# Identity matmuls behind the first 24 TensorE steps of the attention, and two blocks prepared ahead of its cycles in place of four

## The chip, the cores and the metric

The kernel runs on one core of a Trainium2 chip. A core has a matrix engine (TensorE, PE in the profile, with its weight loads listed apart as PEld), a vector engine (VectorE, DVE), a scalar engine (ScalarE, ACT), a general engine (GpSimd, POOL), and a queue that issues most of the DMAs (SyncE, SP). Each works through a list of instructions in order; semaphores make one wait for another. TensorE's clock is throttled and released again by the chip while a program runs; the profile has the granted share in a column PEclk, where 1.00 is the full clock. The metric is device time in microseconds, the median of several executions; lower is better.

## The reference, cut to what matters

The program is one layer of an encoder over 4096 tokens of 1024 features: an RMSNorm, one wide projection, a sparse attention, a pooling branch, gates, and an output projection. The change lies in the attention, which follows an indexer that picks 256 keys for every query:

```python
def block(i):                       # 32 blocks of 128 queries
    iscore = sum_h(relu(qi_h @ ki.T) * wi_h)          # indexer
    iscore = where(key_chunk <= q_chunk, iscore, -inf)
    idx = top_k(iscore, 256)
    s = (q @ k[idx].T) * HEAD_DIM ** -0.5             # 8 heads of 64, 2 key/value heads
    s = where(valid, s, -inf)
    o = softmax(s) @ v[idx]
```

The kernel computes the attention over all keys up to the block's own, with a bias of -1e30 where a key was not picked, which gives the same sums.

## The kernel before, in words

The program has phases: the projection to queries, keys and indexer terms, the indexer with the rest of the projections beside it (until about 2104 us), the attention (2107 us on) and the output phase. In the attention a *unit* is one block of 128 queries and one of the two key/value heads, 64 units in all, and block b has (b + 2) // 2 pairs of key tiles. Scores are formed with a high and a low part of queries and keys, in three products.

What has to be ready before a unit's first softmax tile:

- `keys(b, ...)` loads the rows of two key blocks (`k`). For the first ten blocks TensorE transposes them in one step of eight transposes (`turn_both`, through the helper `turn`, L345), and ScalarE and then VectorE copy them out of PSUM to `kh` and `kl` (`share`, L1273).
- `queries(b, ...)` loads the rows of the queries (`q`) and a copy of the bias (`bis`). In `turn_part` TensorE transposes eight heads in one step; blocks 0 to 3 have two such steps, and each is copied out by ScalarE and then VectorE to `qh` and `ql` (L1273). Block 4 and the later ones have one, and two DMAs move the rest.
- `maxima(u, t, ...)` multiplies queries and keys once (L1441, `ps` or `st`), VectorE takes the maximum of each row (L1450) into `mf`, copies it to `mz` (L1465), and `turn_maxima` has TensorE transpose it (four transposes into `pt`, L345); ScalarE puts it into `qm` (L1488). The softmax subtracts it.

Then come, for each pair of tiles, `softmax` (the logits in four products, L1509, into `st`), `weigh` (VectorE adds the transposed bias, L1522, into `tt`; ScalarE takes the exponential, L1521), `values` (L1561, into `pv`), and GpSimd's running sum of the weights.

The transposes, the first maxima and the logits share one PSUM ring, `st`, of two buffers; a step of TensorE that writes a buffer waits until the other engines have read what was in it. `ps` has one buffer. `pv` has two halves of one bank.

The order of the work is not the scheduler's of the framework. The code declares steps (`Plan.add`) with an engine, an estimated cost, a key and what they follow; `Plan.run` plays a clock with these costs, and each time an engine is free it takes the ready step with the smallest key whose buffers have room. The instructions are written out in the order in which this picks them. All steps of TensorE in the attention go through `chain`, which ties each to the one declared before it (`last_pe`), so that TensorE's order is the order of the declarations. Before the main loop, a short loop declares keys, queries and maxima of the first four blocks (`for b in range(min(WB, QB))`, QB = 4), with keys from -100 on; the main loop then declares whatever comes due, cycle by cycle.

Of the kernel before, what the change touches and what calls it, by code (L numbers as in the profile page):

```python
# [43 lines left out]
WB = 10  # L44
# [7 lines left out]
CHF = 0.16  # L52
TB = 8
MX = 8
FD = 4
FE = 2
AL = 10
# [3 lines left out]
QB = 4  # L61
# [71 lines left out]
class Plan:  # L133
# [11 lines left out]
    def new(self, name, role=None):  # L145
        return Tile_(name, role)
# [104 lines left out]
class K:  # L251
# [898 lines left out]
    def phase_attention(self):  # L1150
# [17 lines left out]
        v, act, pe, gp = nc.vector, nc.scalar, nc.tensor, nc.gpsimd  # L1168
# [27 lines left out]
        pl = Plan()  # L1196
        new = pl.new
# [15 lines left out]

        def chain(cost, key, fn, after=(), new=(), use=(), form=0):

            last_pe[0] = pl.add("pe", cost, key, fn, [*after, last_pe[0]], new, use, form)
            return last_pe[0]

        def wide(b):

# [6 lines left out]
        def landed(key, after, use):  # L1227

            s = pl.add("dma", 0.01, key, lambda: None, [after])
            return pl.add("nil", 0.0, key - 500, lambda: None, [s], use=use)  # L1230

        def keys(b, base):

            k4 = new("k4")

            def load():
                two = slice(b * P, (b + 2) * P)
                sp_dma(k4.t.rearrange("p t g c -> p t (g c)").bitcast(F32),
                       self.hlD[two, H_K:H_QI].rearrange("(t p) c -> p t c", p=P))

            def load_values():
                sp_dma(vv[:, b:b + 2], self.rowD[slice(b * P, (b + 2) * P), R_V - R_QI:].rearrange("(t p) c -> p t c", p=P))
            ld = pl.add("dma", 0.8, base - 8, load, use=[k4])
            VV[b // 2] = pl.add("dma", 0.5, base + 9, load_values, [ld])
            if b < WB:
                turn_both(b, k4, ld, base + 1)
                return
            k4.users += 2
            for n in range(2):
                turns.append((base + 1 + n, lambda n=n: turn_keys(b, n, k4, ld, base + 1 + n)))  # L1250

        def turn_both(b, k4, ld, key):

            s = wide(b)
            cols = slice(b // 2 * P, b // 2 * P + P)
            half = [slice(0, 64), slice(64, P)]

            def turn():
                for n in range(2):
                    for i in range(2):  # L1260
                        for g in range(2):
                            self.turn(four(s)[:, n, 2 * i + g], k4.t[:, n, g, 64 * i:64 * i + 128])
            t = chain(0.9, key, turn, [ld], [s], [k4], form=2)

            def put(n, copy):
                copy(kh[half[n], :, cols], four(s)[half[n], n, 2 * n:2 * n + 2])
                copy(kl[half[n], :, cols], four(s)[half[n], n, 2 - 2 * n:4 - 2 * n])
            share(key, put, 0.8, t, [s], b)
            K_[b] = K_[b + 1] = pl.add("nil", 0.0, key - 500, lambda: None, list(parts_of))
# [13 lines left out]
        def turn_keys(b, n, k4, ld, key):  # L1283

            pt = new("pt")
            half, cols = slice(64 * n, 64 * n + 64), slice(b // 2 * P, b // 2 * P + P)

            def turn():
                for i in range(2):
                    for g in range(2):  # L1290
                        self.turn(pt.t[:, 2 * i + g], k4.t[:, n, g, 64 * i:64 * i + 128])
            t = chain(0.3, key, turn, [ld], use=[pt, k4], form=2)
            k4.users -= 1

            def put():
                act.activation(kh[half, :, cols], pt.t[half, 2 * n:2 * n + 2], AF.Copy)
                act.activation(kl[half, :, cols], pt.t[half, 2 - 2 * n:4 - 2 * n], AF.Copy)
            K_[b + n] = pl.add("act", 0.53, key, put, [t], use=[pt])
# [47 lines left out]
        def turn_part(b, n, q2, qh, ql, ld, done, key):  # L1346
# [3 lines left out]
            def turn():  # L1350
                for h in range(8):
                    self.turn(four(s)[:, h // 4, h % 4], q2.t[:, P * h + 64 * n:P * h + 64 * n + P])
            t = chain(0.9, key, turn, [ld], [s], [q2], form=2)

            def put(f, copy):
# [52 lines left out]
        def flip(b):  # L1408

            bt = new("bTs" if b < 8 else "bT")  # L1410

            def turn():
                if b < 2:
                    gp.memset(bt.t[:, 0:b + 1], 0.0)
                    gp.memset(bt.t[64:, b, 0:64], -1e30)
                else:
                    nc.sync.dma_start_transpose(bt.t[:, 0:b + 1], self.biasD[b, :, :P * (b + 1)])
            BT[b] = bt, pl.add("pool" if b < 2 else "dma", 0.3 if b < 2 else 0.8, at[2 * b] - BTL - (40 if b < 8 else 0), turn, last_bt, use=[bt])
            last_bt[:] = [BT[b][1]]

        def maxima(u, t, key):
# [39 lines left out]
            if g == 1:  # L1461
                landed(key, last, [bias])
            if b < MX:
                mz = new("mz")
# [163 lines left out]
        last_pe, last_ve, last_lb, last_bt, summed, wait_sums, odd, parts_of = [None], [None], [], [], {}, [], [0], []  # L1628
# [9 lines left out]
            tiles += [(lo + n * t / n_of[u], u, t) for t in range(n_of[u])]  # L1638
        base = [(at[2 * b - 1] if b else -2) - 2 * LEADP - AP for b in range(NB)]
        first, b_next, ready, x = 0, 0, 0, -2  # L1640
        for b in range(min(WB, QB)):
            if b % 2 == 0:
                keys(b, -100 + b)
                first = b + 2
            queries(b, -100 + b)
            flip(b)
            b_next = b + 1
            for q in [q for q in tiles if q[1] // 2 == b - 1]:
                tiles.remove(q)
                maxima(q[1], q[2], -100 + b)  # L1650
        while ready < len(pairs) or wait_sums:
            key = 2 * x
# [55 lines left out]
        s = pl.add("dma", 0.1, at[-1] - 60, room, done)  # L1708
# [8 lines left out]
        for i in range(2):  # L1717
# [4 lines left out]
            for m in (2 * i, 2 * i + 1):  # L1722
                ps = new("st")

                def mm(ps=ps, m=m):
# [8 lines left out]
                    use=[g, ps])  # L1734
# [358 lines left out]
```

## Time and profile before

| | us |
|---|---|
| time, median of 3 runs | 4171.93 (4167.88 to 4175.81) |
| the profiled execution, its own time | 4178.22 |
| its span, from first to last instruction | 4176.1 |
| mean granted TensorE clock in it | 0.983 |
| PE busy over the span | 4026.6 |
| DVE busy | 3237.4 |
| ACT busy | 2290.4 |
| POOL busy | 2080.1 |

In the lines of the profile, a group reads: line of the kernel, engine, operation, output<-input, shapes, count | busy time, mean time of one. A timeline row starts with the start in us from the span's beginning, then the duration of the merged instructions; what stands in brackets is the time for which the engine sat idle before it, and who released it. In the rows of stretches of time, each engine has its busy time and in brackets the number of its instructions; PEclk, the DMA share and GB/s stand at the end.

### The profile page before, as it was taken

The page shows a single profiled execution, that of the slowest core. Times are in us where ns is not written, and L with a number is a line of the kernel's source. Part 1 is how long each engine was busy: PE and PEld are TensorE (multiplying, and loading weights), DVE is VectorE, ACT ScalarE, POOL GpSimd, SP SyncE. Part 2 cuts the span into 40 slices and gives each one's busy share as a digit, 9 for nine tenths or more (in the row PEclk, how much of TensorE's full clock was granted, in tenths as well). Part 3 has the DMA queues.
Part 4 walks back from the last instruction along what each step waited for, and adds up shares of the span by engine and source line. Part 5 has one row for each costly group of instructions (what it writes and reads, how often), then busy time and mean ns, then how long its engine had stood idle before and what let it go on. Part 6 is the DMA issues. An engine that isn't in the chain of part 4 may idle for free. (4 is left out here: it accounts for less than half of the span.)

```text
span 4176.1 us, 75863 instructions
## 1 busy us (share of the span) xinstructions
PE 4026.6 (96%) x28418; PEld 3334.1 (80%) x28419; DVE 3237.4 (78%) x6520; ACT 2290.4 (55%) x3419; POOL 2080.1 (50%) x1797
## 2 busy tenths in 40 slices
PE   8999899999999999999979999999999999999999
PEld 7888799999899899999966666666666666887887
DVE  6455578888888878778778999999999995556644
ACT  4444578777787778887645555555454443111221
POOL 3455312312323423100017889999999995334653
PEclk9999999999999999999979999999999999999999
DMA  6666644544545444756663433332322215887543
GB/s 215 239 239 236 222 159 153 193 163 159 187 160 169 158 169 162 239 209 210 228 150 74 84 76 66 59 60 54 64 43 53 32 21 165 276 264 233 196 156 121
DMA packets 516142, 638.86 MB, mean 153 GB/s; under 512 B 230398, under 2 KB 381882, under 8 KB 511675
## 3 DMA queue, kind: packets, MB, share of 16 engines
q1 hardware_dynamic: 490682, 610.78, 46.2%
q10 hardware_dynamic: 25088, 23.21, 2.5%
q8 instruction: 224, 3.67, 0.4%
q14 instruction: 148, 1.20, 0.1%
HBM read 409.70 MB, written 192.28 MB: 144 GB/s over the span
## 5 line engine op out<-in xcount | busy, mean ns | idle before, releaser
L1061 PE MATMUL pd<-h,wgh 128*128 128x256 f32 x3584 | 1018.9, 284 | 1.5 <-DVE zsm L981 0.8
L1062 PE MATMUL pd<-h,wgh 128*128 128x256 f32 x3584 | 1012.9, 283 | 0.0
L1063 PE MATMUL pd<-h,wgl 128*128 128x256 f32 x3584 | 1012.2, 282 | 0.5 <-POOL wgl L1028 0.5
L1540 POOL TENSOR_TENSOR acc<-acc,tt 128x1024 f32<-128x1024 f32 x388 | 927.5, 2391 | 65.4 <-ACT tt L1521 38.7
L1521 ACT ACTIVATE tt<-tt 128x1024 f32<-128x1024 f32 (+1 forms) x544 | 561.0, 1034 | 551.8 <-DVE tt L1522 521.1
L779 DVE SCALAR_TENSOR_TENSOR ring<-rl,wi,ring 128x1024 f32<-128x1024 f32 (+7 forms) x624 | 692.2, 1150 | 16.2 <-ACT rl L777 13.9
L1061 PEld LDWEIGHTS pd<-h,wgh 128*128 128x128 f32 x3584 | 681.0, 190 | 20.6 <-DVE zsm L981 1.0
L1062 PEld LDWEIGHTS pd<-h,wgh 128*128 128x128 f32 x3584 | 681.8, 190 | 15.9 <-DMA h<-hD 0.3
L1063 PEld LDWEIGHTS pd<-h,wgl 128*128 128x128 f32 x3584 | 681.7, 190 | 0.7 <-POOL wgl L1028 0.7
L777 ACT ACTIVATE rl<-ps 128x1024 f32<-128x1024 f32 (+7 forms) x624 | 540.3, 889 | 151.7 <-DVE ring L779 54.7
L1522 DVE TENSOR_TENSOR tt<-st,bT 128x1024 f32<-128x1024 f32 (+1 forms) x504 | 601.4, 1195 | 17.0 <-PE st L1509 15.4
L1561 PE MATMUL pv<-tt,vv 128*64 128x256 f32 x4224 | 522.3, 389 | 1.4 <-ACT ov L1582 1.4
L864 ACT ACTIVATE sg<-ring,tk 128x2048 fp8e4<-128x2048 f32 (+8 forms) x322 | 485.3, 1509 | 43.6 <-DVE tk L852 19.8
L1450 DVE CUSTOM_DVE_ANT_1 jk<-ps,bias,mf 128x1024 bf16<-128x1024 f32 (+3 forms) x408 | 470.1, 1152 | 20.3 <-PE ps L1441 18.4
L1561 PEld LDWEIGHTS pv<-tt,vv 128*64 128x64 f32 x4224 | 288.6, 138 | 171.5 <-issue 40.9
L774 PE MATMUL ps<-kis,qT 128*128 128x512 f32 (+3 forms) x1136 | 343.0, 385 | 29.1 <-ACT rl L777 28.8
L1865 PE MATMUL p<-g,w 128*128 128x512 f32 x1488 | 345.5, 394 | 1.7 <-DVE g L1788 1.7
L972 POOL COPY halo<-u 128x16 f32<-128x16 f32 x64 | 29.0, 453 | 635.3 <-ACT u L966 623.0
L1865 PEld LDWEIGHTS p<-g,w 128*128 128x128 f32 x1488 | 279.3, 188 | 67.7 <-DVE g L1788 2.1
L2014 PE MATMUL p<-w,g 128*128 128x512 f32 x1344 | 315.0, 397 | 3.9 <-ACT g L2018 3.9
L2014 PEld LDWEIGHTS p<-w,g 128*128 128x128 f32 x1344 | 254.5, 189 | 64.3 <-ACT g L2018 4.3
L1441 PE MATMUL ps<-kh,qh 64*128 64x512 f32 (+3 forms) x1320 | 266.0, 419 | 30.2 <-DVE mf L1450 27.5
(341 smaller groups left out, 7107.1 us busy)
## 6 DMA issues: line engine op xcount, KB each, us to landing
h<-hD SPq DMA_DIRECT2D x192, 1024.0 KB
g<-gD SPq DMA_DIRECT2D x80, 512.0 KB
hlD<-rhl SPq DMA_DIRECT2D x32, 1216.0 KB
gD<-sgm SPq DMA_DIRECT2D x256, 128.0 KB
x<-x SPq DMA_DIRECT2D x32, 512.0 KB
wraw<-w_in SPq DMA_DIRECT2D x32, 512.0 KB
hD<-hh SPq DMA_DIRECT2D x32, 512.0 KB
hD<-hl SPq DMA_DIRECT2D x32, 512.0 KB
```

What stands on the lines that cost most here:

```text
L777: r = pl.add("act", 0.05 + n * 0.834e-3, k_, lambda ps=ps, rl=rl, n=n: act.activation(rl.t[:, :n], ps.t[:, :n], AF.Relu), [m], use=[ps, rl])
L779: prev[o] = pl.add("dve", 0.1 + n * 1.04e-3, k_, lambda rl=rl, o=o, n=n, h=h: v.scalar_tensor_tensor(acc[:, o:o + n], rl.t[:, :n], self.wi ...
L864: mine.append(pl.add("act", 0.28 + m * 0.834e-3, key, lambda sg=sg, o=o, m=m, e=e, j=j, b=b: act.activation(sg.t[:, o:o + m], where[b][:, ...
L1061: pe.matmul(out, wh.t[:, k], r1, start=(k == 0), stop=False)
L1062: pe.matmul(out, wh.t[:, k], r2, start=False, stop=False)
L1063: pe.matmul(out, wl.t[:, k], r1, start=False, stop=(k == KT - 1))
L1521: act.activation(tt.t[:, 0:n], tt.t[:, 0:n], AF.Exp)
L1522: ad = last_ve[0] = pl.add("dve", 0.07 + 0.54 * n, key, lambda: v.tensor_tensor(tt.t[:, 0:n], s.t[:, 0:n], bc(bt.t[:, 2 * p:2 * p + n, Non ...
L1540: gp.tensor_tensor(acc.t, first, tt.t, op=OP.add)
L1561: pe.matmul(pv.t[64 * f:64 * f + 64], vv[:, k, 64 * g:64 * g + 64], T[u, p].t[:, k % 2, 2 * f:2 * f + 2], start=(k == 0), stop=(k == b))
L1865: pe.matmul(p.t, blk[i].t[:, k, ms], two(x[k // 2][j].t, F32R)[:, k % 2], start=(k == i == j == 0), stop=(k == 3 and i == 1))
L2014: pe.matmul(p.t, quarter(Q.t, x, F32R)[:, k], blk[y].t[:, k], start=(fresh and k == x == y == 0), stop=(k == 3 and x == 1), skip_group_che ...
```

## The change

Behind each of the first 24 steps that go through `chain`, a further step is declared: eight matmuls with the 128 x 128 identity (`identr`) as both operands, written to one half of `pv`, which nobody reads before it is overwritten. The next step of the chain follows it, so TensorE does it between the two. 24 packs of eight are 192 matmuls. Their estimated cost in the plan is 0.06 x 8 = 0.48 us.

The loop ahead of the main loop now runs over two blocks in place of four. Blocks 2 and 3 are declared by the main loop, with the keys that its rule gives.

```diff
+WARM = 8
+WARMS = 24
...
         def chain(cost, key, fn, after=(), new=(), use=(), form=0):

-            last_pe[0] = pl.add("pe", cost, key, fn, [*after, last_pe[0]], new, use, form)
-            return last_pe[0]
+            s = last_pe[0] = pl.add("pe", cost, key, fn, [*after, last_pe[0]], new, use, form)
+            if warm:
+                x = pl.new("pv")
+                last_pe[0] = pl.add("pe", 0.06 * warm.pop(), key, lambda: keep_busy(x), [s], use=[x])
+            return s
+
+        warm = [WARM] * WARMS
+
+        def keep_busy(x):
+
+            for _ in range(WARM):
+                pe.matmul(x.t[:, 0], self.identr, self.identr, start=True, stop=True)
...
-        for b in range(min(WB, QB)):
+        for b in range(2):
```

How TensorE's order moves is seen at two places. The first is the begin of the attention on PE: the transposes of the first keys (`k_27854`) and of the queries of blocks 0 and 1 (`q_27863`, `q_27872`), and the first maxima. Before:

```order
L345 MATMUL st_27877<-identr,k_27854 128x128 x8
L345 MATMUL st_27889<-identr,q_27863 128x128 x8
L345 MATMUL st_27905<-identr,q_27863 128x128 x8
L345 MATMUL st_27927<-identr,q_27872 128x128 x8
L345 MATMUL st_27944<-identr,q_27872 128x128 x8
L1441 MATMUL st_27960<-kh,qh_27914 128x128 x8
```

And with the change, where L345 is L347, L1441 is L1453 (lines stand two further down above `chain` and twelve below it), and L1229 is the line of the identity matmuls:

```order
L347 MATMUL st_27877<-identr,k_27854 128x128 x8
L1229 MATMUL pv<-identr 128x128 x8
L347 MATMUL st_27904<-identr,q_27863 128x128 x8
L1229 MATMUL pv<-identr 128x128 x8
L347 MATMUL st_27928<-identr,q_27863 128x128 x8
L1229 MATMUL pv<-identr 128x128 x8
L347 MATMUL st_27954<-identr,q_27872 128x128 x8
L1229 MATMUL pv<-identr 128x128 x8
L347 MATMUL st_27978<-identr,q_27872 128x128 x8
L1229 MATMUL pv<-identr 128x128 x8
L1453 MATMUL st_28003<-kh,qh_27922 128x128 x8
L1229 MATMUL pv<-identr 128x128 x8
```

Nothing here has changed places; a pack stands behind every step.

The second place is a little further on, on PE too: queries of block 2 and of block 3, and maxima of block 1 (with its queries, `qh_27940`) between them. Before:

```order
L345 MATMUL st_28018<-identr,q_27921 128x128 x8
L345 MATMUL st_28031<-identr,q_27921 128x128 x8
L1441 MATMUL st_28050<-kh,qh_27940 128x128 x8
L345 MATMUL pt_28062<-identr,mz_27846 66x128 x4
L1441 MATMUL ps_28068<-kh,qh_27940 128x128 x8
L345 MATMUL pt_28094<-identr,mz_27845 66x128 x4
L345 MATMUL st_28101<-identr,q_27955 128x128 x8
L345 MATMUL st_28116<-identr,q_27955 128x128 x8
```

With the change (block 1's queries are `qh_27972` here, and block 3's rows `q_27987`):

```order
L347 MATMUL st_28120<-identr,q_27938 128x128 x8
L1229 MATMUL pv<-identr 128x128 x8
L347 MATMUL st_28145<-identr,q_27987 128x128 x8
L1229 MATMUL pv<-identr 128x128 x8
L347 MATMUL st_28168<-identr,q_27987 128x128 x8
L1229 MATMUL pv<-identr 128x128 x8
L1453 MATMUL st_28192<-kh,qh_27972 128x128 x8
L1229 MATMUL pv<-identr 128x128 x8
L347 MATMUL pt_28209<-identr,mz_27846 66x128 x4
L1229 MATMUL pv<-identr 128x128 x8
L1453 MATMUL ps_28232<-kh,qh_27972 128x128 x8
```

The two transposing steps of block 3 now come before the maxima of block 1, not behind them; VectorE's and ScalarE's copies of them move in the same way. On SP's queue, one load of values (`vv`) goes ahead of the two loads of block 2's bias (`bis`), and the two loads of block 3's bias go ahead of a load of values and the load of block 4's queries. The 24th pack stands behind the first logits. The transposes of block 2's second maximum, two transposing steps and two logits further on, stand five steps of TensorE later than before; from there on, the order of the instructions on each engine is the same as before, to the end of the program.

## The prediction

> **What bounds the kernel now.** I read the page's slices first, then the busy times of single stretches, then the instructions of the one stage that the change touches. The page's slices:
>
> ```profile
> span 4176.1 us, 75863 instructions
> PE   8999899999999999999979999999999999999999
> DVE  6455578888888878778778999999999995556644
> PEclk9999999999999999999979999999999999999999
> ```
>
> TensorE is busy throughout, and there is one dip in its clock, in slice 21 (2088 to 2192 us): the begin of the attention. Further on, the attention is held by VectorE, with TensorE just under it:
>
> ```profile
> 2400.00:2800.00 400.00, 391.30 (x3174) 257.55 (x3176) 392.68 (x582) 209.76 (x256) 364.06 (x171) 1.00 0.34 65
> ```
>
> PE has 391.30 and DVE 392.68 of 400 us, so what the begin gains or loses before VectorE's queue is full is kept to the end: the instructions and their order behind it are the same. The begin, in stretches (us, then PE, PEld, DVE, ACT, POOL, then PEclk):
>
> ```profile
> 2107.68:2155.47 47.79, 32.64 (x204) 26.97 (x202) 32.01 (x95) 18.26 (x35) 6.41 (x18) 0.50 0.53 146
> 2110.30:2142.70 32.40, 20.28 (x145) 17.52 (x145) 23.84 (x76) 13.07 (x23) 3.85 (x15) 0.50 0.49 141
> 2110.30:2155.40 45.10, 31.83 (x196) 26.34 (x196) 31.14 (x93) 16.64 (x30) 3.85 (x15) 0.50 0.50 136
> 2169.12:2175.95 6.83, 5.63 (x31) 3.62 (x32) 3.21 (x9) 3.11 (x7) 2.68 (x3) 0.50 0.89 188
> 2203.26:2210.08 6.82, 5.92 (x30) 3.76 (x32) 2.41 (x6) 3.69 (x10) 3.41 (x2) 0.50 0.76 187
> ```
>
> For 47.8 us the clock is half, and it is half again in two spells of 6.83 us. Neither TensorE (20.28 of 32.40) nor VectorE (23.84) is full in the first part: they wait for each other. VectorE's waits between 2113 and 2158 us:
>
> ```profile
> DVE qh L1273 <- ACT ql L1273: 5.0, 3, 2.8
> DVE tt L1522 <- PE st L1509: 2.8, 1, 2.8
> DVE ql L1376 <- ACT qh L1372: 1.7, 1, 1.7
> DVE jk L1450 <- PE st L1509: 1.5, 1, 1.5
> DVE qh L1273 <- PE st L345: 1.2, 1, 1.2
> DVE kh L1273 <- ACT kl L1273: 0.9, 1, 0.9
> DVE ql L1273 <- ACT qh L1273: 0.5, 1, 0.5
> ```
>
> These are 13.6 us (in all, times, longest). The longest of the first row, 2.8, belongs to the load of the first queries and would stay. 10.8 us are thus the ceiling of a gain, if VectorE never waited again.
>
> **What raises the clock.** The ends of the half-clock spells lie whole multiples of 3.413 us apart (47.79 is 14 of them, 6.83 two, and another such spell, at 1561.55, begins 160 of them before 2107.68), so the chip seems to judge stretches of a fixed grid. I compared such stretches; the second fence has the same ones for the transposes (L345) alone.
>
> ```profile
> 1561.55:1564.96 3.41, 2.92 (x11) 2.73 (x12) 3.41 (x4) 2.38 (x3) 1.37 (x2) 0.50 0.80 294
> 2148.64:2152.06 3.42, 3.10 (x20) 2.65 (x20) 1.66 (x5) 1.83 (x4) 0.00 (x0) 0.50 0.73 151
> 2152.06:2155.47 3.41, 3.11 (x17) 2.01 (x13) 3.33 (x9) 0.07 (x1) 0.00 (x0) 0.50 1.06 254
> 2199.84:2203.26 3.42, 2.51 (x14) 1.58 (x14) 3.42 (x5) 2.45 (x3) 0.39 (x1) 1.00 0.00 0
> 2916.64:2920.06 3.42, 1.80 (x16) 1.06 (x12) 3.06 (x5) 1.63 (x2) 3.34 (x2) 1.00 0.00 0
> ```
>
> ```profile
> 2110.30:2142.70 32.40, 13.62 (x96) 11.82 (x96) 0.50 0.49 141
> 2148.64:2152.06 3.42, 1.23 (x8) 1.07 (x8) 0.50 0.73 151
> 2199.84:2203.26 3.42, 0.87 (x8) 0.73 (x8) 1.00 0.00 0
> ```
>
> 2.92 us of matmuls (1561) and 3.11 (2152) were each followed by the full clock, but 3.10 us of which 1.23 were transposes (2148) were not. 2.51 us with 0.87 of transposes (2199) lost the full clock, while 1.80 us without any (2916) kept it. So transposes do not seem to count: without them the sums are 2.92 and 3.06 (raised), 1.87 (not raised), 1.64 (lost), 1.80 (kept). To raise, some 85% of a stretch must be other matmuls; to keep, some 52%. The Trainium skill says the same (TensorE: Matmul & The Clock Gate, Part 4: PE-mode transpose): transposes do not count as busy for the clock in the same way. By that rule too, the stretches at 2148 and 2199 come out as the trace has them. In the first part 13.62 of PE's 20.28 us are transposes, which is why the clock stays down there.
>
> **The change, part by part.** *A pack's price.* The trace has no identity matmul that is not a transpose. The nearest rows are the transposes with the same identity, and the short maxima (and, in the second fence, the time of one transpose at half clock, least/median/most, and its mean at full clock):
>
> ```profile
> 2110.36 2.24 PE L345 MATMUL st<-identr,q 128*128 128x128 f32 x16 [1.92 <-DMA q<-hlD]
> 2115.89 1.23 PE L345 MATMUL st<-identr,q 128*128 128x128 f32 x8 [0.16 <-DVE qh L1273]
> 2118.53 1.12 PE L1441 MATMUL st<-kh,qh 64*128 64x128 f32 x8 [1.41 <-DVE ql L1273]
> 2119.41 1.09 PE L1441 MATMUL ps<-kh,qh 64*128 64x128 f32 x8
> 2168.24 0.88 PE L345 MATMUL st<-identr,k 128*128 128x128 f32 x8
> 2180.51 0.50 PE L1441 MATMUL ps<-kh,qh 64*128 64x384 f32 x4
> 2180.84 0.45 PE L1509 MATMUL st<-qh,kh 64*128 64x512 f32 x2
> ```
>
> ```profile
> L345 PE MATMUL st<-identr,q x72: 308/328/341, 2110.4 to 2149.9; 128*128 128x128 f32 x72
> L345 PE MATMUL st<-identr,q 128*128 128x128 f32 x8 | 0.9, 253 | 0.1
> ```
>
> At half clock, 16 transposes take 2.24 us with the last one's 0.33 of latency, so 0.127 each, and eight short maxima take 2119.41 - 2118.53 = 0.88, so 0.11. A pack is 0.88 to 1.02 us; I take 0.95. At full clock, four maxima take 2180.84 - 2180.51 = 0.33, or 0.083 each, and eight transposes 0.88 with 0.25 of latency, or 0.09; a pack is 0.66 to 0.72 us, and I take 0.69.
>
> *First part (2110.3 to 2142.7).* The first pack falls in the 1.92 us in which PE waits for the queries, and the last behind the first logits; 22 lie in this part. At half clock they need 22 x 0.95 = 20.9 us, and PE has 32.4 - 20.28 = 12.1 us idle: 8.8 us would not fit. At full clock the old work shrinks to about 0.7 (0.09 to 0.127), 14.2 us, and the packs are 15.2: 29.4 in all, which fits. So all hangs on how soon the clock rises. Among the turns a pack stands behind every eight transposes (0.95 to 1.0), so other matmuls have about half of each stretch, which neither raises nor reliably keeps the clock. Behind them the pack after the last of these turns, maxima, pack, maxima and pack of block 0 make 0.95 x 3 + 1.1 x 2 = 5.1 us in one piece, enough for a stretch of 3.41 in most phases of the free-running count: the clock rises near 2122, may be lost again among the five turns of blocks 2 and 3, and rises for good among the maxima of blocks 1 and 2, near 2138. That is some 12 + 11 = 23 us at half clock. PE's 20.28 + 20.9 = 41.2 us of half-clock work then last 23 + 18.2 x 0.7 = 35.8 us, 3.4 longer than the 32.4. VectorE's waits for ScalarE's copies of the same turn (first row of its waits) do not vanish with it; with 0.6 us for them the first logits start about 4 us late.
>
> *Second part (2142.7 to 2155.4).* PE has 31.83 - 20.28 = 11.55 us of work in 12.7, DVE 31.14 - 23.84 = 7.3. It is all at half clock now; the first logits, and the mean of one logits product in the groups by line of 2109 to 2155 and of 2176 to 2199:
>
> ```profile
> 2142.69 0.79 PE L1509 MATMUL st<-qh,kh 64*128 64x512 f32 x1
> L1509 PE MATMUL st<-ql,kh 64*128 64x512 f32 x6 | 2.5, 626 | 0.0
> L1509 PE MATMUL st<-ql,kh 64*128 64x512 f32 x17 | 3.9, 391 | 0.0
> ```
>
> 391 against 626 ns is a ratio of 0.62, so PE's part shrinks by at most 0.38 x 11.55 = 4.4 us. VectorE can follow where it waits for PE or for what PE hands to ScalarE: 2.8 + 1.5 + 1.7 = 6.0 us of waits, of which 0.38 is 2.3. I take 2.5. What stays hidden is VectorE's own 7.3.
>
> *The two blocks.* The 16 transposes of block 3 and their copies go ahead of block 1's maxima; none is added. VectorE and ScalarE work on the moved copies while PE does its packs. If that cover is gone, the price is one more wait like the 0.9 and 0.5 us that VectorE has now behind such copies. On SP one load of values goes ahead of the bias of block 2:
>
> ```profile
> 2112.87 0.37 SPq L1242 DMA_DIRECT2D vv<-rowD  x1
> 2136.62 0.69 DVE L1450 CUSTOM_DVE_ANT_1 jk<-st,bis 128x512 bf16<-128x512 f32 x1
> ```
>
> It costs 0.37 us of issue, and the bias is first read at 2136.62, over 20 us later. Block 3's bias goes ahead of block 4's queries, whose load waits for block 2's turns anyway. I put all this at nothing, with 1 us either way.
>
> The sum is +4 - 2.5 = +1.5 us. It is made on a span of 4176.1 in an execution of 4178.22, which is 6.3 above the median of the runs (4171.93), and is the same few instructions in each; so I carry it over: **4173.4 us**. With the clock up from the first stretch it would be about -3, and with the two later spells moved or not, 0.38 x (5.63 + 5.92) = 4.4 either way; the forecast's own range is 4167 to 4179. A measurement of this kernel tells no change from one of 0.2%, 8.3 us.
>
> **The rivals.** *A. Any work counts (same side).* If packs and transposes alike raise the clock, it is full from the second stretch, near 2117. PE then needs 29.4 us and two stretches at half clock add 0.3 x 6.8 = 2.0; it stays under 32.4, VectorE's chain sets the first logits (0.5 later, since a ready step waits for up to 0.69 us and is shorter by 1.23 - 0.88 = 0.35), and the second part gives 3: -2.5, 4169.4. Against it stands the stretch at 2148. The general rule of the Trainium skill would have it so (TensorE: Matmul & The Clock Gate, Part 1: The HAM clock gate: full after one busy window of about 3.4 us). By that rule, the trace agrees on the length, and the stretch at 2148 departs from the rest of it.
>
> *B. The full gain (faster).* The clock is up from the first stretch, packs fall only into idle time, and VectorE's waits nearly vanish: -9 of the ceiling of 10.8, 4163. Or -4.5 from the begin and -4.4 from the two later spells, if the earlier phase takes them away. Against it: at full clock PE would have 32.4 - 14.2 = 18.2 us idle in the first part, and the packs would have to lie in 15.2 of them without one being in the way.
>
> *C. The packs keep the clock down (slower).* If the five-microsecond piece of block 0 falls across two stretches, and the maxima of blocks 1 and 2, with their four transposes in between, stay under 85%, then the first part runs at half clock to its end: the 8.8 us that do not fit are paid, and the second part gains nothing, as it starts late and cold: 4171.9 + 8.8 = 4181. It takes the whole first part at half clock; at two thirds of it, 23 us, the sum is the forecast's. For it: the free-running phase, and 13.62 of 20.28. Against it: with packs the share of other matmuls there is (6.66 + 20.9) / 41.2 = 67%, and well above among the maxima.
>
> *D. The change does not do what it says:* eight times the same identity count for the clock no more than a transpose does. Then the packs cost as in C.
>
> **How the numbers follow.** Forecast 0.46, A 0.29, B 0.14, C with D 0.11. Forecast and A lie within 0.2%, B is faster, C slower: 0.14 / 0.75 / 0.11; a little of the forecast's low end goes to B's side, so 0.15, 0.74, 0.11. The range reaches from B's value to just under C's: 4163 to 4180.5.
>
> **What would show it.** PEclk between 2110 and 2120 us still 0.50, then 1.00 near 2122 and from 2138 on; TensorE nearly without idle time in the first part; the first logits (2142.69 now) 3 to 5 us later, and the products with values that start at 2156 now one or two us later. Rival A shows the clock up by 2118 and the first logits within 1 us of before; B shows them earlier; C shows 0.50 up to 2150. A pack over 1.1 us at half clock, or one that waits for `pv`, would make the sum wrong, as would a change of the spells after 2169 by more than one.

## The result, and the profile after

The changed kernel takes 4196.41 us (median of 4 runs, 4195.68 to 4200.73), against 4172.01 for the kernel before beside it: a ratio of 1.0061, with a 95% interval of 1.005 to 1.0073. It is 24 us slower. The prediction was 4173.4 us, in a range that ended at 4180.5.

The profiled execution took 4195.94 us with a span of 4193.8. Its page:

```profile
span 4193.8 us, 76250 instructions
PE   8999899999999999999999999999999999999999
DVE  6455678888888887777659999999999995556654
PEclk9999999999999999999969999999999999999999
```

Slice 21 of the 40 (2097 to 2202 us) holds the begin of the attention: VectorE falls to 5 there, and the granted clock to 6. (The attention began some 8 us earlier in this execution; that differs from execution to execution, 2097 to 2107 us over the runs here, so times below count from the first transposes.) The stretches of time that answer to those of before (us, then PE, PEld, DVE, ACT, POOL with their instructions, then PEclk, the DMA share and GB/s), and the same for the identity matmuls alone (PE, PEld):

```profile
2099.46:2174.55 75.09, 72.98 (x388) 67.74 (x390) 30.80 (x92) 18.50 (x34) 6.64 (x19) 0.50 0.31 89
2188.20:2195.03 6.83, 5.65 (x32) 4.16 (x34) 4.65 (x12) 2.75 (x7) 3.29 (x4) 0.50 0.40 103
2113.11:2116.53 3.42, 3.42 (x20) 3.18 (x20) 1.94 (x6) 1.18 (x2) 0.00 (x0) 0.50 0.52 163
2400.00:2800.00 400.00, 391.38 (x3158) 257.32 (x3156) 389.28 (x583) 209.15 (x259) 360.91 (x170) 0.99 0.35 68
```

```profile
2099.46:2174.55 75.09, 46.52 (x192) 42.87 (x192) 0.50 0.31 89
```

The half-clock spell lasts 75.09 us where it lasted 47.79. TensorE is busy for 72.98 of them, VectorE for 30.80: the begin is now bound by TensorE, and for 46.52 us of it a pack is running. Further on, from 2400 us, the busy times are as before: 391.38 and 389.28 of 400 us. The first rows on TensorE, and the first logits:

```profile
2099.47 1.23 PE L347 MATMUL st<-identr,k 128*128 128x128 f32 x8 [2.04 <-DMA k<-hlD]
2100.49 1.93 PE L1229 MATMUL pv<-identr 128*128 128x128 f32 x8
2103.65 1.23 PE L347 MATMUL st<-identr,q 128*128 128x128 f32 x8 [1.23 <-DMA q<-hlD]
2104.68 1.93 PE L1229 MATMUL pv<-identr 128*128 128x128 f32 x8
2106.41 1.21 PE L347 MATMUL st<-identr,q 128*128 128x128 f32 x8
2107.42 1.93 PE L1229 MATMUL pv<-identr 128*128 128x128 f32 x8
...
2161.37 0.79 PE L1521 MATMUL st<-qh,kh 64*128 64x512 f32 x1
```

A pack holds TensorE for 2106.41 - 2104.68 = 1.73 us, 0.216 a matmul; eight transposes take 1.01 (2107.42 - 2106.41). The first transposes of the kernel before:

```profile
2107.37 1.07 PE L345 MATMUL st<-identr,k 128*128 128x128 f32 x8 [2.07 <-DMA k<-hlD]
```

The first logits come 2161.37 - 2099.47 = 61.9 us after the first transposes; before it was 2142.69 - 2107.37 = 35.3. These 26.6 us are the loss, and most of it is kept to the end: from the first transposes to the end of the span it is 4193.8 - 2099.5 = 2094.3 us, against 2068.7, so 25.6 more. That the two agree to 1 us is partly luck. In this figure two profiled executions of one kernel (e1 and e11 below) differ by 7.1 us, and the profile of the changed kernel has one half-clock spell between 2180 and 2300 us (2188.20), where the one of before had three between 2160 and 2300 us.

VectorE's waits from 2103 to 2172 us show the turned tables (total, times, longest); before, VectorE's waits for matmuls ahead of the maxima (L1450 there, L1462 here) were 1.5 us in the list:

```profile
DVE qh L1285 <- ACT ql L1285: 9.0, 4, 3.9
DVE jk L1462 <- PE ps L1453: 7.0, 4, 3.3
DVE jk L1462 <- PE st L1453: 6.7, 4, 3.2
```

### The profile page after: what moved, and what is told of

It is laid out like the page before. It is cut to its first block, busy times and chain, and to the rows that moved or that the text cites. A ratio compares the mean times of both kernels' runs of the same rounds, so it can differ in the third digit from the quotient of the medians.

```text
span 4193.8 us, 76250 instructions
## 1 busy us (share of the span) xinstructions
PE 4057.6 (97%) x28610; PEld 3365.1 (80%) x28611; DVE 3237.0 (77%) x6520; ACT 2290.9 (55%) x3419; POOL 2084.6 (50%) x1797
## 4 chain that ended last, share of the span: by engine, by line
PE 62%; DVE 13%; issue 7%; POOL 6%; ACT 4%; DMA 4%; SPq 1%; ACTq 0%; DVEq 0%; POOLq 0%
PE pv L1573 8%; PE st L1521 7%; PE pd L1063 7%; PE pd L1064 7%; PE pd L1065 7%; PE p L2026 7%; PE p L1877 7%; PE ps L776 4%; DVE jk L1462 4%; PE ps L1453 3%; ACT sg L866 2%; POOL row L431 1%; DVE ring L781 1%; DVE tt L1534 1%; PE pt L347 1%
## 5 line engine op out<-in xcount | busy, mean ns | idle before, releaser
L1462 DVE CUSTOM_DVE_ANT_1 jk<-ps,bias,mf 128x1024 bf16<-128x1024 f32 (+3 forms) x408 | 469.4, 1151 | 21.2 <-PE ps L1453 19.7
L1453 PE MATMUL ps<-kh,qh 64*128 64x512 f32 (+3 forms) x1320 | 265.5, 419 | 28.8 <-DVE mf L1462 26.1
```

What stands on the lines that cost most here:

```text
L1462: v.tensor_tensor_reduce(out=jk.t[:, :2 * (hi - lo) * P].rearrange("p (t n) -> p t n", t=2), in0=flat().rearrange("p (t n) -> p t n", t=2) ...
```

## The experiments

Each of these is the changed kernel with one edit; e6, e7 and e8 have theirs on top of that of e4, and e10 and e11 are e4 and e1 run again. "Logits" is the time from the first transposes to the first logits (35.3 us before, 61.9 with the change); "half" is the length of the half-clock spell in which the attention begins. Both are from the profiled execution. Time is the median of the runs, beside that of the kernel before on the same chip.

| | time | before beside it | ratio, 95% | logits | half |
|---|---|---|---|---|---|
| the change | 4196.41 | 4172.01 | 1.0061 [1.005, 1.0073] | 61.9 | 75.1 |
| e1 two blocks, no packs | 4167.2 | 4172.11 | 0.9988 [0.9978, 0.9997] | 32.6 | 44.4 |
| e2 packs, four blocks | 4197.38 | 4172.11 | 1.0062 [1.0043, 1.0081] | 62.8 | 75.1 |
| e3 packs of 256 columns | 4175.92 | 4172.11 | 1.0014 [1.0003, 1.0024] | 40.7 | 6.8 |
| e4 packs in bfloat16 | 4165.12 | 4172.11 | 0.9985 [0.9976, 0.9995] | 33.7 | 6.8 |
| e5 packs of transposes | 4167.64 | 4172.27 | 0.9993 [0.9983, 1.0002] | 35.8 | 10.2 |
| e6 bfloat16, 64 rows | 4180.87 | 4172.27 | 1.0024 [1.0014, 1.0034] | 42.8 | 54.6 |
| e7 bfloat16, four blocks | 4169.24 | 4172.27 | 0.9993 [0.9982, 1.0004] | 35.0 | 6.8 |
| e8 ten bfloat16 packs | 4168.0 | 4172.27 | 0.9995 [0.9986, 1.0005] | 32.6 | 6.8, then 23.9 |
| e9 four matmuls a pack | 4178.5 | 4170.23 | 1.0016 [1.0007, 1.0025] | 44.3 | 58.0 |
| e10 = e4 again | 4167.07 | 4170.23 | 0.9988 [0.9979, 0.9997] | 33.0 | 6.8 |
| e11 = e1 again | 4167.14 | 4170.23 | 0.9991 [0.9982, 1.0] | 33.9 | 44.4 |
| e12 64 columns streamed | 4200.64 | 4171.54 | 1.0064 [1.0046, 1.0082] | 62.0 | 75.1 |
| e13 64 columns of weights | 4167.4 | 4171.54 | 0.9992 [0.9982, 1.0002] | 34.1 | 6.8 |

### Which of the two edits

```diff
e1: -WARMS = 24
    +WARMS = 0
e2: -        for b in range(2):
    +        for b in range(min(WB, QB)):
```

> The change without its packs: the first loop over two blocks, no identity matmuls. Theory (the packs cost all of it): within 0.2% of the kernel before, 4168 to 4177, the half-clock spell at the begin of the attention 45 to 50 us long as before. Rival (the two blocks of preparation are what costs, because block 3's turns push the maxima of block 1 back): slower by 10 us or more, 4182 and up, with VectorE's waits behind the moved copies longer.

> The packs alone, with four blocks prepared as before. Theory: as slow as the whole change, 4193 to 4200, a pack 1.75 to 1.95 us at half clock and the half-clock spell 70 us or longer. Rival (the loss needs both parts): at least 10 us faster than the whole change.

The packs alone give the whole loss (25 us). The other order alone gives none; it is 4.9 us under before here (0.8 under its expected range) and 3.1 in e11, with the clock half for about as long as before. With the packs the order makes no difference that can be told: 4196.41 and 4197.38.

### What a matmul of a pack costs

```diff
e3:  -                pe.matmul(x.t[:, 0], self.identr, self.identr, ...)
     +                pe.matmul(x.t, self.identr, bc(self.identr[:, None], [P, 2, P]), ...)
e4:  +        identb = sp.tile([P, P], BF, name="identb")
     +        v.tensor_copy(identb, self.identr.bitcast(F32))
     ...
     +                pe.matmul(x.t[:, 0], identb, identb, ...)
```

> The whole change, but each of the eight matmuls of a pack streams the identity twice, 256 columns in place of 128. Theory S (a 128-column matmul of this type takes two cycles per column, and the clock is granted by the share of a stretch in which columns really stream, transposes apart): a pack takes the same 1.7 to 1.95 us at half clock with twice the columns, the clock rises at the first stretch without transposes (8 to 20 us after the first turn), packs then take about 0.95 us, and the time falls to 4170 to 4182. Rival D (identity data, which are nearly all zeros, do not count for the clock): half clock for 70 us or more, 4193 to 4200. Rival R (price by rows: twice the columns, twice the time): a pack of 3.4 us, 4230 or more.

> The whole change with the identity in bf16 in the packs, eight matmuls of 128 columns as before (one more copy of 128x128 on VectorE at the begin). Theory S: one cycle per column, a pack of 0.86 to 1.0 us at half clock, columns streaming all through it; the clock rises at a stretch among the maxima of block 0 or of blocks 1 and 2, 4166 to 4178, which is what the prediction had worked out for its own price. Rival D: the packs cost 0.9 us each but the clock stays at half, 4178 to 4186. Rival P (the price lies in reading the identity as both operands, not in its type): 1.75 to 1.95 us a pack and 4193 to 4200.

The second pack and the transposes behind it, of e3 and then of e4 (both still at half clock):

```profile
2101.09 2.04 PE L1229 MATMUL pv<-identr 128*128 128x256 f32 x8
2102.93 1.18 PE L347 MATMUL st<-identr,q 128*128 128x128 f32 x8
```

```profile
2106.99 1.08 PE L1231 MATMUL pv<-identb 128*128 128x128 bf16 x8
2107.83 1.24 PE L347 MATMUL st<-identr,q 128*128 128x128 f32 x8
```

With 256 columns a pack takes 1.84 us, 0.23 a matmul: twice the columns for nearly the same time. In bfloat16 it takes 0.84, 0.105 a matmul, and the time, 4165.12, is 0.9 under the expected range. Both raise the clock within two stretches, where e1 has the same transposes without the packs and stays down for 44.4 us: products with the identity do count for it. What remained was why 128 columns of fp32r (the 32-bit type of `identr`) take twice the time: the load of the weights, or the streaming. Two more kernels halve the one and the other:

```diff
e12: +                pe.matmul(x.t[:, 0, :64], self.identr, self.identr[:, :64], ...)
e13: +                pe.matmul(x.t[:64, 0], self.identr[:, :64], self.identr, ...)
```

> What a pack's 0.213 us a matmul is spent on. Here each matmul streams 64 columns of the identity in place of 128, with the same 128 x 128 weights. Theory (the load of plain fp32r weights sets the pace: the loads of the packs and of the maxima take 0.32 us, those of the transposes 0.18, in rows of the changed kernel): a pack still takes 1.7 us, the clock stays half for some 75 us, and the time is 4190 to 4200. Rival (fp32r streams a narrow operand at half pace): 0.9 us a pack, and the loss that four matmuls in a pack gave, 4174 to 4184.

> The counterpart: each matmul loads 64 columns of the identity as weights in place of 128, and streams 128. Theory (the load sets the pace): a pack takes 0.9 us, the loads some 0.2 each; half of the array is filled for all of the time, so the clock stays half for 40 to 65 us, 4174 to 4184. Rival (the streaming sets it): still 1.7 us a pack, 4190 to 4200.

A pack of e12, and one of e13, each with the transposes behind it:

```profile
2106.49 1.88 PE L1229 MATMUL pv<-identr 128*128 128x64 f32 x8
2108.18 1.25 PE L347 MATMUL st<-identr,q 128*128 128x128 f32 x8
```

```profile
2108.04 1.07 PE L1229 MATMUL pv<-identr 128*64 128x128 f32 x8
2108.91 1.22 PE L347 MATMUL st<-identr,q 128*128 128x128 f32 x8
```

With half the columns a pack still takes 1.69 us; with half the weights it takes 0.87. So the load sets the pace: plain fp32r weights of 128 columns take 0.21 us at half clock. The price of e12 came as the theory of the load had it, and the time 0.6 us over its range. Of e13 the price came so, but both theories had the clock stay down, and it rose after 6.8 us; the time is therefore 4167.4 and not 4174 to 4184. That belongs to the next question.

The loads could have been read in the trace of before. The groups of weight loads there, 2107 to 2143 us, and in the changed kernel, 2099 to 2174 us (busy time and mean ns of one stand behind the bar):

```profile
L345 PEld LDWEIGHTS st<-identr,q 128*128 128x128 f32 x64 | 8.5, 183 | 5.2 <-issue 3.2 <-ACT qh L1273 2.1
L1441 PEld LDWEIGHTS ps<-kh,qh 64*128 64x128 f32 x24 | 3.0, 322 | 2.0 <-issue 2.0
```

```profile
L1229 PEld LDWEIGHTS pv<-identr 128*128 128x128 f32 x192 | 42.9, 328 | 2.0 <-issue 1.5
L347 PEld LDWEIGHTS st<-identr,q 128*128 128x128 f32 x72 | 9.6, 182 | 2.4 <-issue 1.4 <-PE st L347 1.0
```

A load for a transpose lasts 183 ns, one for a maximum 322 ns, and a pack's is of the second kind (328).

The last of this group asks whether it is the length of the packs, or that there are 24 more steps:

```diff
e9: -WARM = 8
    +WARM = 4
```

> The changed kernel with four identity matmuls in a pack in place of eight. Theory (0.213 us apiece at half clock, half of the array filled): a pack takes 0.85 us, the clock stays half for 40 to 65 us as with eight, and the loss is about that of the half-row packs, which last as long: logits 39 to 46 us after the first transposes, 4175 to 4183. Rival (the loss of 24 us comes with 24 more steps and their waits, not with their length): more than half of it stays, 4184 or more.

The loss is 8.3 us and not 24, with the same number of steps: what costs is their length. It is less than half for half the length because TensorE's idle time of before takes the first 12 us. A pack takes 0.87 us (2106.14 to 2107.01), and 22 of them less 12.1 make 7.0; from the first transposes of the queries to the first logits it is 2145.14 - 2105.11 = 40.0 us, against 2142.69 - 2110.36 = 32.3, so 7.7 more. The other 1.3 of the 9.0 us by which the logits are later lie in front of it, in the wait for the load of the queries.

### What raises the clock

```diff
e5: -                pe.matmul(x.t[:, 0], self.identr, self.identr, ...)
    +                self.turn(x.t[:, 0], self.identr)
e6 (on e4): +                pe.matmul(x.t[:, 0], identb[:64], identb[:64], ...)
```

> The packs are eight transposes of the identity in place of eight plain matmuls with it, on two blocks ahead; nothing else differs from the changed kernel. Theory (a stretch is judged by the share in which columns pass through the whole array, transposes included; a pack of plain fp32r matmuls of 128 columns fills only half of it and is twice as long as I took): a pack takes 8 x 0.127 = 1.0 us at half clock and about 0.7 at full, the clock rises with the second or third stretch, it is half for 6.8 to 14 us, the first logits come 33 to 38 us after the first transposes, and the time is 4163 to 4171. Rival (transposes do not count, as my prediction read the trace): up to block 0's maxima TensorE does hardly anything but transposes, so the clock is half for 40 us or more; 22 packs of 1.0 us against 12 us of idle time put the first logits 43 us or more after the first transposes, and the time is 4174 to 4183.

> The packs are bfloat16 and use only 64 of the 128 rows of the identity, on two blocks ahead: each takes as long as a whole bfloat16 pack (0.84 to 1.08 us at half clock), and fills half of the array. Theory (rows times columns count): the clock stays half for 40 to 65 us, and this is what my prediction's price of 0.95 us gives with the clock kept down: 22 x 0.95 = 21 us against 12 of idle time, so the first logits come 38 to 46 us after the first transposes, and the time is 4170 to 4180. Rival (streaming without a pause counts, whatever the rows): as with whole bfloat16 packs, half for 6.8 us, logits at 34, 4162 to 4168.

The first three stretches of e5 and what follows, and then the same for the transposes' line alone (PE and PEld):

```profile
2100.91:2104.32 3.41, 2.24 (x16) 2.09 (x16) 0.51 (x3) 2.18 (x4) 2.52 (x6) 0.50 0.89 261
2104.32:2107.74 3.42, 2.83 (x23) 2.86 (x23) 0.73 (x3) 1.18 (x2) 3.30 (x10) 0.50 0.89 285
2107.74:2111.15 3.41, 3.41 (x29) 3.38 (x27) 2.49 (x5) 2.00 (x4) 0.81 (x4) 0.50 0.68 181
2111.15:2148.70 37.55, 32.19 (x334) 28.22 (x332) 27.99 (x87) 13.37 (x25) 0.20 (x1) 1.00 0.45 125
```

```profile
2100.91:2104.32 3.41, 2.24 (x16) 2.09 (x16) 0.50 0.89 261
2104.32:2107.74 3.42, 2.83 (x23) 2.86 (x23) 0.50 0.89 285
2107.74:2111.15 3.41, 3.41 (x29) 3.38 (x27) 0.50 0.68 181
```

The counts are the same in both, so TensorE did nothing but transposes, and the clock rose after the third stretch. Transposes count. (A count in a row takes in matmuls that began before the stretch and still run; of the 29, 26 began in it.)

A pack of e6 and the transposes behind it (0.96 us, all at half clock), its whole half-clock spell, one stretch of it, and the stretch of e13 that ended with the full clock:

```profile
2108.49 1.03 PE L1231 MATMUL pv<-identb 64*128 64x128 bf16 x8
2109.45 1.26 PE L347 MATMUL st<-identr,q 128*128 128x128 f32 x8
```

```profile
2102.48:2157.09 54.61, 52.33 (x387) 44.61 (x387) 31.00 (x92) 17.82 (x34) 6.23 (x17) 0.50 0.42 123
2112.72:2116.13 3.41, 3.41 (x34) 3.34 (x32) 2.61 (x7) 1.18 (x2) 0.00 (x0) 0.50 0.74 209
```

```profile
2107.07:2110.49 3.42, 3.42 (x30) 3.42 (x31) 0.97 (x2) 1.52 (x3) 2.88 (x13) 0.50 0.63 195
```

TensorE is busy without a gap in the stretch of e6 and of the changed kernel (2113.11: 3.42 of 3.42), and both stay at half clock. So busy time does not decide. What fits is how much of a stretch passes data into all 128 rows. 128 columns pass in at most 0.105 us at half clock (e4). In the changed kernel's stretch 19 matmuls begin, 8 of them maxima of 64 rows. If those count half, the data pass for (11 + 4) x 0.105 = 1.6 of 3.42 us, 0.46, since the loads take the rest. In e6's, 32 matmuls begin, all of 64 rows: 32 x 0.105 / 2 = 1.7, 0.49. Not raised either. In the three of e5, where 16, 23 and 26 begin, it is 0.49, 0.71 and 0.80, and the third raised it; in e13's, where 29 begin, 29 x 0.105 = 3.05, 0.89, raised, though half of the columns of the array stood empty in the packs. So rows count and columns do not, which is why e13 missed; the share that raises lies between about 0.7 and 0.8 in these runs.

The pair of stretches in the kernel before on which the prediction's rule rested cannot be told apart in this way. In the one from 2148.64 begin 8 transposes, 4 maxima of 256 columns and 8 logits of 512, these twelve with 64 rows. But the last two of the logits begin at its very end:

```profile
2151.99 0.63 PE L1509 MATMUL st<-qm,neg 64*128 64x512 f32 x2
```

So most of their data pass in the next stretch. A count by time, with 0.105 us for 128 columns, gives 0.76 for the stretch from 2148.64, which did not raise the clock, and 0.73 for the one from 2152.06, which did. What tipped the second stays open. The same count over all 523 half-clock stretches of the fifteen traces bears the rule out: the 281 that left the clock at half have at most 0.77, and of the 242 that raised it 237 have 0.78 or more and five have 0.69 to 0.75, this one among them. That 64 rows count exactly half was assumed in the count, and no run tries it by itself.

### What the full clock is worth

```diff
e7 (on e4): -        for b in range(2):
            +        for b in range(min(WB, QB)):
e8 (on e4): -WARMS = 24
            +WARMS = 10
```

> Whole bfloat16 packs, and four blocks ahead as before: the clock's worth without the other order. If the two edits are independent (two blocks alone gave about -5 us), this is 2 us under before, 4167 to 4172, with the clock half for 6.8 to 14 us. If the raised clock is what the run with both gained by, and the order gives nothing beside it, 4162 to 4167.

> Whole bfloat16 packs behind the first ten steps only, two blocks ahead. Theory (raising needs about 0.7 of a stretch, keeping less than half): the clock is raised by the first packs as with 24, may be lost once more behind the tenth, and the time is that with 24 or up to 2 us less, 4161 to 4167. Rival (the clock lives on the packs): it falls back for 20 us or more behind the tenth, and the time is that of two blocks alone, 4166 to 4170.

> The kernel with whole bfloat16 packs and two blocks once more, with more rounds, to settle whether it beats the kernel before: 4163 to 4168, 4 to 9 us under before; if the first result was luck, within 2 us of before.

> Two blocks ahead without any packs once more, on the same chip as the bfloat16 packs: 4165 to 4170. If early full clock is worth what the difference of the first two results says, 2 us over the bfloat16 packs; if it is worth nothing, within 1 us of them.

In e4 the clock is half for 6.83 us and full for the 37.5 behind them:

```profile
2102.45:2109.28 6.83, 5.19 (x44) 4.96 (x44) 1.61 (x4) 3.04 (x7) 6.22 (x17) 0.50 0.76 244
2109.30:2146.80 37.50, 29.69 (x355) 24.57 (x352) 29.84 (x91) 15.16 (x28) 0.20 (x1) 1.00 0.52 140
```

The first logits come 33.7 us after the first transposes; in e1, with the clock half, 32.6. e10 and e11, on one chip, have 4167.07 and 4167.14. On the chip of e1 and e4 it was 4167.2 and 4165.12. So the full clock in the begin, less what its packs cost, is worth 0 to 2 us, which these runs do not tell from nothing. TensorE is busy for 29.69 of the 37.50 us and VectorE for 29.84, so neither holds the other all the time. VectorE's waits between 2105 and 2136 us are 6.5 us for ScalarE's copies and 0.9 for transposes in e4, and 7.7 and 1.2 in e1, so the full clock takes little of them away; which handover sets the pace there no run settles. e7, the same without the other order, came where independent edits put it, 3.0 us under before, with an interval that holds 1. In e8 the rival was right: the clock fell back for 23.89 us behind the tenth pack, and 4168.0 is in its range and not in the theory's.

The kernels of e1 and e11 (two blocks and no packs), and of e4 and e10, are the only ones under before whose interval stays at or below 1: by 3 to 7 us, about 0.1%, less than the 0.2% that the prediction called the bound of what can be told. Their medians lie under those of both kernels, and of the two the one without packs is the simpler.

## Why the prediction was wrong

**The bound.** It was right to within the scatter of these figures: what the begin gains or loses is kept to the end. The first logits are 26.6 us late, and the time is longer by 25.6 from the first transposes to the end and by 24.4 in the medians.

**A pack's price** is the step that failed. "A pack is 0.88 to 1.02 us; I take 0.95" rested on rows of the two kinds that escape the price: transposes, whose loads are short (183 ns), and maxima of 64 rows, which the code issues in turn on the two halves of the rows. Eight of these take 0.88 us although each load lasts 322 ns, about as long as a pack's, so their loads seem to overlap more; no run here tries that by itself. The nearest rows were near in shape and not in what sets the pace, and the two ends of the range lay on the same side. The measured pack takes 1.73, and over 1.1 was a sign of being wrong that the prediction named itself. With 1.73 its own sum for the first part, all at half clock, is 22 x 1.73 - 12.1 = 26.0 us. Measured there were 25.4: from the first transposes of the queries to the first logits it is 2161.37 - 2103.65 = 57.7 us, against 2142.69 - 2110.36 = 32.3. The other 1.2 of the 26.6 lie in front of it, in the wait for the load of the queries.

**The price at full clock** never came up, since no pack of the changed kernel ran there.

**The clock's rule** failed too, and on its own. "Transposes do not count" is refuted by e5, and "some 85% of a stretch must be other matmuls" by the changed kernel itself: the stretch from 2113.11 was busy to the full with maxima and packs, and left the clock at half. The Trainium skill's sentence on this (TensorE: Matmul & The Clock Gate, Part 4: PE-mode transpose), that a transpose does not count as busy in the same way, disagrees with e5: 10.2 us of nothing but transposes raised the clock. The Trainium skill's general rule (TensorE: Matmul & The Clock Gate, Part 1: The HAM clock gate) has the clock rise after one busy stretch; the length of 3.41 us agrees, "busy" does not: 72.98 of 75.09 us were busy at 0.50. The measurements decide.

**"8.8 us would not fit"** was near for its price: e6's packs last 0.96 us at half clock, the clock stays down, its first logits come 42.8 - 35.3 = 7.5 us later, and it came to 4180.87 (0.9 over its expected range), 8.6 over before, where rival C had 8.8. The reason that C gave (a piece that falls across two stretches) is not what kept the clock down, and with the price doubled C's way costs 26 us.

**The second part** (-2.5) was lost: it still ran at half clock. From the first logits to the first product with the values it took 13.5 us before and 15.7 now, with the 24th pack in it.

**The two blocks** at 0 ± 1 was too cautious on the gain without packs: 3 to 5 us (e11, e1).

**Rivals A and B.** A had the full clock after one or two stretches and the two blocks at nothing. The nearest to that is e7, with four blocks: 4169.24 where A had 4169.4, though e7's interval holds 1. With two blocks, as in the change, the same packs came to 4165.12 and 4167.07 (e4, e10). So A was near for packs that raise the clock, in part by luck; these packs did not raise it. B's -9 came in no run. **D** (the identity does not count) is rejected by e3 and e4.

## What to carry to other kernels

Before an instruction is priced at that of a neighbour in the trace, look at the row that sets the neighbour's pace: here the weight loads stood in a list of their own, 183 against 322 ns, and the matmul rows alone (328 and 423 ns, mostly latency) hid it. Work that is added to hold a clock up must itself be of the kind that counts, and an engine that reads busy may be waiting for its weights. And first ask what the full clock would be worth where three engines hand work on to each other: here it was worth nothing that could be measured.

## What the runs showed of the hardware that was not expected

- A plain fp32r matmul of 128 rows with 128 columns of new weights takes 0.21 us at half clock, whether it streams 64, 128 or (0.23) 256 columns (e12, the change, e3). With 64 columns of weights it takes 0.109 (e13), in bfloat16 0.105 (e4), and as a transpose 0.126 (eight in 1.01).
- TensorE was 97% busy for 75 us and kept the half clock. What raised it was the share of a 3.41-us stretch in which data pass into all 128 rows, from between 0.7 and 0.8 on; transposes count, products with the identity count, time in which the next matmul waits for its load does not, 64 rows count for less (half fits), and empty columns of the array cost nothing (e5, e4, the change, e6, e13). Of 523 half-clock stretches five raised the clock with a little less.
